# Two feed-forward tiles side by side in the opening wave instead of three, with weights loaded earlier and three pieces of work spread later

## The chip, the cores and the metric

The kernel runs on one NeuronCore of a Trainium2 chip. The metric is the time of one execution in microseconds (us) on the device; the time before is the median of three runs.

Engines are named as the profile names them: PE is TensorE (matmuls), PEld its weight load, DVE is VectorE, ACT is ScalarE, POOL is GpSimd, SP is SyncE, which here only issues DMAs. A name with a q (SPq, ACTq) is the engine's queue of instructions that wait, branch or issue.

## The reference

One layer of a diffusion backbone over 256 latent and 256 context tokens of width 2048, all in float32:

```python
mod = silu(c) @ w_ada + b_ada              # 9 chunks of 2048; the same for the context's condition
x   = x   + 0.5 * gate * swiglu(rms_norm(x)   * (1 + scale) + shift, w_ffn1_up, w_ffn1_down)
ctx = ctx + 0.5 * gate * swiglu(rms_norm(ctx) * (1 + scale) + shift, w_ffn1_up, w_ffn1_down)
h   = modulate(rms_norm(x), ...)           # and the same for ctx
q, k, v, hy = split(h @ w_in);  kc, vc from the context
attn = softmax(rope(q) [kc; k]^T) [vc; v]  # 8 query heads, 2 key heads of 128
hyo  = hyena(hy, filters)                  # short conv, gate, long conv by an implicit filter, gate
x   = x + gate * concat(rms_norm(attn), rms_norm(hyo)) @ w_out
x   = x + 0.5 * gate * swiglu(modulate(rms_norm(x)), w_ffn2_up, w_ffn2_down)
```

The feed-forward width is 5632. The hyena filters come from a small sine network and are used by their spectrum.

## The kernel before

**Arithmetic.** A float32 product is made of three matmuls in a shorter float format: every operand is split into a high and a low part (`hi`, `lo`), and hi x hi, hi x lo and lo x hi are summed in PSUM (`mm3`). `weight` loads a piece of 0.5 MB into `raw` by SP's queue (four buffers), ACT casts it to `whi` (L199) and DVE makes `wlo` = raw - whi (L201); `whi` and `wlo` have three buffers each. One piece of `up` is 24 matmuls of 512 columns (256 latent and 256 context tokens side by side).

**Order.** The framework puts the instructions of each engine in an order by a planner with its own costs, starting from the order in which the program states them; `tc.issue_after(x)` forces an instruction behind another. The engines then run their orders and wait for each other by semaphores. DMAs issued by SP stand in SP's order, so one that waits for a free buffer holds up those behind it.

**The start.** The tokens `xs` (16 loads) are squared on ACT and summed on DVE; PE sums over partitions (L244), DVE and ACT make 1/rms (`rstd_from`, with a Sqrt on ACT, L231, ahead of which ACT loads a function table), and `spread_row` puts it into all partitions (L255 to L257). `keep_awake` runs matmuls without use meanwhile. The shift and scale of the first feed-forward come from PE: `ada_row(d)` loads 2 MB of `w_ada` for d-tile d (128 of the 2048 columns) into `wrow` (four buffers of 1 MB), multiplies (L163), and `ada_col(d)` copies the row (L170), turns it (L173) and writes the two columns of `mod` (L175, L177).

**The wave.** There are 44 ff tiles of 128 columns. The first `WAVE` = 3 run side by side, because their input `h` comes into being d-tile by d-tile: for d = 0 to 15, `ada_row(d + 2)`, `ada_col(d + 1)`, `wave_h(d)` (L523 on DVE, L525 on ACT for hi, L527 on DVE for lo), then six matmuls (L208 to L210) for each of the three tiles. Their pieces of weights are loaded at d = 0, 4, 8 and 12, when they are needed. The third tile's two PSUM banks come from the `pb` pool, in which the banks of `ada_row` and of the filter also lie. Between the tiles `next(steps)` runs pieces of `filter_spectrum`: three layers of the sine network (matmul L379, DVE L381 to L386, Sin on ACT L388), then four blocks of 256 channels (Exp L414, matmul L417, L418 to L431 on DVE with Abs on ACT L425, L434 to L439, spectrum L445 to L450).

**After the wave.** `f1.up(j)` runs the other ff tiles one by one in four pieces, and after each four of them `f1.down` adds their part of the output. Behind each piece `ada_hook` puts products for the other chunks of the modulation on DVE (`ada_dve`, L136), which need the condition rows `crow`; these are loaded by SP and put through Silu right behind the wave.

**Mixing.** The last `down` runs first for the context tokens, then for the latents; `mix_input` makes the inputs of the projections meanwhile, driven by the hook and by `KV_PLAN`: `rstd_steps` squares (L266) and, one step on, makes 1/rms and spreads it together with the first `h`. Later `group_in` splits the outputs of attention and hyena for the output projection and sums their squares; `out_unit(g, b)` multiplies group g by a quarter of the output's columns, and `out_add` multiplies by 1/rms and the gate (L955) and adds to the stream (L956). The hyena group's `group_in` stands as a whole behind the first unit. Behind the last unit, 16 matmuls without use keep PE awake, and the second feed-forward's input is normed and turned (L1005).

Of the kernel before, what the change touches and what calls it, by code (L numbers as in the profile page):

```python
# [18 lines left out]
P = 128  # L19
D = 2048  # L20
# [11 lines left out]
WAVE = 3  # L32
# [21 lines left out]
def hybrid_layer_kernel(ctx: ExitStack, tc: tile.TileContext, a):  # L54
# [137 lines left out]
    def weight(src, shape, eng=None, behind=None):  # L192
        raw = T(wp, shape, "raw", bufs=4)
        load = nc.sync.dma_start(raw, src)
        if done[0]:
            last_load[0] = load
        hi = T(wp, shape, "whi", F32R, 3)
        lo = T(wp, shape, "wlo", F32R, 3)
        S.copy(hi, raw)  # L199
        if behind is None:  # L200
            (eng or V).tensor_sub(lo, raw, hi.bitcast(F32))  # L201
        else:
            with tc.issue_after(behind.ins):
                V.tensor_sub(lo, raw, hi.bitcast(F32))
# [32 lines left out]
    def row_rstd(tiles, n, y, between=None):  # L237


# [7 lines left out]
        with ExitStack() as order:  # L247
            if between:
                with tc.issue_after(last.ins):
                    order.enter_context(tc.issue_after(between().ins))  # L250
            return spread_row(nt, r_, y)

    def spread_row(nt, r_, y):
# [5 lines left out]
    def rstd_steps(pairs, n, y):  # L259

        todo_, acc = [], None
        for q, t in enumerate(pairs):
            last = q == len(pairs) - 1
            sq = (tmp if last or acc is not None else tmp2)((P, 2, L))
            for part in ((0, 1) if last else (slice(0, 2),)):
                S.activation(sq[:, part, :], t[:, part, :], AF.Square)  # L266
            if last:
                todo_.append(sq)
# [6 lines left out]
        row_rstd([[t_[:, j, t * P : (t + 1) * P] for t_ in todo_ for j in range(2)] for t in range(2)], n, y)  # L275
# [22 lines left out]
    class Ffn:  # L298
# [12 lines left out]
        def piece(self, j, kq, ps2, eng=None):  # L311
            whi, wlo = weight(self.wup[j, kq], (P, 4, 2, P), eng)
# [181 lines left out]
    for i in range(2):  # L494
        for q, t in enumerate(xs[i]):
            sq = U((P, 2, L))
            S.activation(sq, t, AF.Square)
            if q:
                last_sq = V.tensor_add(accs[i], accs[i], sq)
            else:  # L500
                accs.append(sq)
    spin = PA()
# [11 lines left out]
    with tc.issue_after(last_sq.ins):  # L514
        with tc.issue_after(awake.ins):
            spread = row_rstd([[accs[i][:, j, t * P : (t + 1) * P] for j in range(2)] for i in range(2) for t in range(2)],
                     D, rs.rearrange("p i l -> p (i l)"), lambda: ada_row(0))
# [26 lines left out]
    for d in range(KT):  # L544
# [6 lines left out]
        for j in range(WAVE):  # L551
            if d and d % 4 == 0:
                w[j] = weight(f1.wup[j, d // 4], (P, 4, 2, P))
            mm = f1.tile(d, d % 4, w[j], wave[j])
            with ExitStack() as first:
# [3 lines left out]
                if j < 2 or d < 3:  # L559
                    next(steps, None)  # L560
    for _ in steps:
        pass
# [5 lines left out]
    crow = [T(adap, (P, D), f"crow{i}", bufs=1) for i in range(2)]  # L568
    for i in range(2):
        nc.sync.dma_start(crow[i], a["crow"][i : i + 1, :].partition_broadcast(P))  # L570
        S.activation(crow[i], crow[i], AF.Silu)
    f1.hook = ada_hook
# [601 lines left out]
```

## Time and profile before

| | |
|---|---|
| median of 3 runs | 2696.45 us (2695.83 to 2697.5) |
| profiled execution | 2693.7 us, span from first to last instruction 2691.9 us |
| mean granted clock of PE | 0.997 of full speed |
| PE busy | 2661.5 us (99%) |
| DVE busy | 1715.6 us (64%) |
| ACT busy | 940.8 us (35%) |
| moved by DMA | 515.43 MB, mean 191 GB/s |

The profile shows one execution. Busy times of PE are modelled and overlap from one matmul to the next, so the distance from start to start says more than the length of one. A wait is the idle time of an engine ahead of an instruction, named by what it waited for last.

### The profile page before, as it was taken

To read this page: it belongs to the slowest core of one execution; us is meant where nothing else is said; L and a number is where in the kernel's file an instruction comes from. 1 tells how busy PE (TensorE), PEld (TensorE's weight loads), DVE (VectorE), ACT (ScalarE), POOL (GpSimd) and SP (SyncE) were. 2 spreads that over 40 slices of the span, in tenths; PEclk is the share of its full clock that TensorE was granted. 3 is DMA by queue.
4 is the path that set the end of the run, shared out by engine and by line. 5 is a ranking of instruction groups with operands and counts; after the bars stand their busy time and mean duration, and the time that the engine had idled before them with its cause. 6 is when DMAs were issued, how large, how long until landed. Compare 5 with 4: busy or idle time off the path is not lost.

```text
span 2691.9 us, 32590 instructions
## 1 busy us (share of the span) xinstructions
PE 2661.5 (99%) x12588; PEld 2187.1 (81%) x12588; DVE 1715.6 (64%) x2687; ACT 940.8 (35%) x1217; POOL 1.0 (0%) x7
## 2 busy tenths in 40 slices
PE   9999999999999999999999999999999999999999
PEld 6678888888888888888888878888888888888887
DVE  5589898976696767443333697788665555554444
ACT  4343222222222222222222455456454444444333
POOL 0000000000000000000000000000000000000000
PEclk9999999999999999999999999999999999999999
DMA  9776666666686665522322455334645555556664
GB/s 368 299 271 216 217 212 229 206 232 212 221 296 235 204 229 208 188 99 94 101 95 95 133 165 188 125 110 157 194 163 190 188 188 189 190 191 203 200 200 157
DMA packets 145395, 515.43 MB, mean 191 GB/s; under 512 B 17303, under 2 KB 21336, under 8 KB 140888
## 3 DMA queue, kind: packets, MB, share of 16 engines
q1 hardware_dynamic: 143464, 510.60, 55.7%
q10 hardware_dynamic: 1776, 2.75, 0.3%
q8 instruction: 99, 1.62, 0.2%
q14 instruction: 56, 0.46, 0.1%
HBM read 509.07 MB, written 4.21 MB: 191 GB/s over the span
## 4 chain that ended last, share of the span: by engine, by line
PE 95%; DVE 3%; DMA 1%; issue 0%; ACT 0%; SPq 0%; ACTq 0%; DVEq 0%
PE pa L210 12%; PE pa L209 12%; PE pa L208 11%; PE pa L940 10%; PE pa L939 10%; PE pa L938 10%; PE pb L208 7%; PE pb L210 7%; PE pb L209 7%; PE pa L216 3%; PE pa L218 2%; PE pb L163 1%; PE pa L652 1%; PE pa L653 1%; PE pa L651 1%; DVE wlo L201 1%
## 5 line engine op out<-in xcount | busy, mean ns | idle before, releaser
L201 DVE TENSOR_TENSOR wlo<-raw,whi 128x1024 fp32r<-128x1024 f32 x645 | 788.1, 1223 | 674.1 <-ACT whi L199 661.6
L199 ACT CAST whi<-raw 128x1024 fp32r<-128x1024 f32 x648 | 681.1, 1052 | 1360.6 <-PE pa L209 495.2
L210 PE MATMUL pa<-u,wlo 128*128 128x512 f32 x1376 | 535.7, 390 | 2.7 <-DVE wlo L201 2.7
L208 PE MATMUL pa<-u,whi 128*128 128x512 f32 x1376 | 536.9, 391 | 1.0 <-ACT u L525 0.9
L209 PE MATMUL pa<-u,whi 128*128 128x512 f32 x1376 | 536.8, 390 | 0.8 <-DVE u L527 0.8
L939 PE MATMUL pa<-wlo,u 128*128 128x512 f32 x1072 | 418.5, 390 | 1.9 <-DVE wlo L201 1.9
L938 PE MATMUL pa<-whi,u 128*128 128x512 f32 x1072 | 419.9, 392 | 0.3 <-ACT u L1010 0.3
L940 PE MATMUL pa<-whi,u 128*128 128x512 f32 x1072 | 418.5, 391 | 0.0
L208 PEld LDWEIGHTS pa<-u,whi 128*128 128x128 f32 x1376 | 258.0, 188 | 58.4 <-issue 3.9
L210 PEld LDWEIGHTS pa<-u,wlo 128*128 128x128 f32 x1376 | 258.1, 188 | 57.3 <-DVE wlo L201 3.8
L209 PEld LDWEIGHTS pa<-u,whi 128*128 128x128 f32 x1376 | 258.4, 188 | 56.7 <-DVE u L527 2.1
L208 PE MATMUL pb<-u,whi 128*128 128x512 f32 (+1 forms) x800 | 299.3, 375 | 0.0
L209 PE MATMUL pb<-u,whi 128*128 128x512 f32 (+1 forms) x800 | 298.1, 373 | 0.0
L210 PE MATMUL pb<-u,wlo 128*128 128x512 f32 (+1 forms) x800 | 298.1, 373 | 0.0
L939 PEld LDWEIGHTS pa<-wlo,u 128*128 128x128 f32 x1072 | 201.8, 188 | 43.1 <-DVE wlo L201 2.0
L940 PEld LDWEIGHTS pa<-whi,u 128*128 128x128 f32 x1072 | 201.5, 188 | 43.0 <-DVE u L1012 1.0
L938 PEld LDWEIGHTS pa<-whi,u 128*128 128x128 f32 x1072 | 201.6, 188 | 41.9 <-ACT u L1010 0.6
L136 DVE CUSTOM_DVE_ANT_0 adas<-adaw,crow,mod 128x1024 bf16<-128x1024 f32 x160 | 205.0, 1281 | 25.4 <-DMA adaw<-in_w_adaT_dram 22.9
L136 DVE CUSTOM_DVE_ANT_0 adas<-adaw,crow,bada 128x1024 bf16<-128x1024 f32 x160 | 204.9, 1280 | 18.0 <-DMA adaw<-in_w_adaT_dram 15.9
L208 PEld LDWEIGHTS pb<-u,whi 128*128 128x128 f32 x800 | 151.2, 189 | 31.0 <-issue 4.8
L210 PEld LDWEIGHTS pb<-u,wlo 128*128 128x128 f32 x800 | 151.2, 189 | 26.9 <-issue 0.8
L209 PEld LDWEIGHTS pb<-u,whi 128*128 128x128 f32 x800 | 151.2, 189 | 26.1
(237 smaller groups left out, 2096.9 us busy)
## 6 DMA issues: line engine op xcount, KB each, us to landing
raw<-in_w_up_dram SPq DMA_DIRECT2D x352, 512.0 KB, 3.3
adaw<-in_w_adaT_dram SPq DMA_DIRECT2D x223, 512.0 KB, 5.1
raw<-in_w_dn_dram SPq DMA_DIRECT2D x184, 512.0 KB, 3.8
wrow<-in_w_ada_dram SPq DMA_DIRECT2D x32, 1024.0 KB, 7.4
raw<-in_w_hy_dram SPq DMA_DIRECT2D x32, 512.0 KB, 3.3
raw<-in_w_o_dram SPq DMA_DIRECT2D x32, 512.0 KB, 4.0
raw<-in_w_kv_dram SPq DMA_DIRECT2D x16, 512.0 KB, 3.7
raw<-in_w_q_dram SPq DMA_DIRECT2D x16, 512.0 KB, 3.3
```

Of the source, the lines that this page charges most:

```text
L136: V.tensor_tensor_reduce(out=sc, in0=t, in1=crow[i][:, b * (D // 2) : (b + 1) * (D // 2)], scale=1.0, scalar=mcol if b else bada[:, n : n ...
L163: last = PE.matmul(bank[g : g + 32, 0 : 2 * P], cs[:, k, :], t[:, k8, :], start=k < 4, stop=k >= KT - 4)
L199: S.copy(hi, raw)
L201: (eng or V).tensor_sub(lo, raw, hi.bitcast(F32))
L208: PE.matmul(ps, w[0], xx[0], start=start, stop=False)
L209: PE.matmul(ps, w[0], xx[1], start=False, stop=False)
L210: return PE.matmul(ps, w[1], xx[0], start=False, stop=stop)
L216: PE.matmul(ps, w[0], x, start=start, stop=stop)
L218: PE.matmul(ps[:, 0, :], w[1], x[:, 0, :], start=False, stop=False)
L938: PE.matmul(ps[t], hi, w[0], start=start, stop=False)
L939: PE.matmul(ps[t], hi, w[1], start=False, stop=False)
L940: last = PE.matmul(ps[t], lo, w[0], start=False, stop=stop)
```

## The change

`WAVE` becomes 2: the third ff tile is made by `f1.up(2)` behind the wave. The weights of the wave's next four d-tiles are loaded into `raw` at the end of d = 1, 5 and 9 (`weight_load`), and `weight` takes them from there at d = 4, 8 and 12. The filter keeps its number of steps: one behind each tile, and one more behind the second tile while d < 3. The condition rows are loaded behind `up(2)`, by ACT's queue, and the hook is set there. `row_rstd` is divided into `token_rstd` (sums and 1/rms) and `spread_row`; in `rstd_steps` a `yield` lies between them, so that the generator has one step more, and one `next(more)` is added before the hook takes over. `root_table` puts a Sqrt of one column behind the last square, so that ACT loads its table there. `group_in` becomes a generator of four steps, and the hyena group's steps stand one behind each of the four units. In `out_unit`, the last of the four pieces finishes token tile 0 before token tile 1, and `out_add` puts token tile 1's product behind token tile 0's sum.

```diff
--- before.py
+++ after.py
@@ -29,7 +29,7 @@
 UPG = FF // 256
 CT = HW // P
 EPS = 1e-6
-WAVE = 3
+WAVE = 2
 ADA_RATE = 1.25
 FILTER_J = 36
 GATE_J = 20
@@ -189,16 +189,21 @@
         V.tensor_sub(lo, src, hi.bitcast(F32))
         return hi, lo
 
-    def weight(src, shape, eng=None, behind=None):
+    def weight_load(src, shape):
         raw = T(wp, shape, "raw", bufs=4)
         load = nc.sync.dma_start(raw, src)
         if done[0]:
             last_load[0] = load
+        return raw
+
+    def weight(src, shape, behind=None, raw=None):
+        if raw is None:
+            raw = weight_load(src, shape)
         hi = T(wp, shape, "whi", F32R, 3)
         lo = T(wp, shape, "wlo", F32R, 3)
         S.copy(hi, raw)
         if behind is None:
-            (eng or V).tensor_sub(lo, raw, hi.bitcast(F32))
+            V.tensor_sub(lo, raw, hi.bitcast(F32))
         else:
             with tc.issue_after(behind.ins):
                 V.tensor_sub(lo, raw, hi.bitcast(F32))
@@ -234,8 +239,12 @@
         V.scalar_tensor_tensor(e, e, -0.5, m, op0=ALU.mult, op1=ALU.mult)
         return V.scalar_tensor_tensor(y, e, 1.5, y, op0=ALU.add, op1=ALU.mult)
 
-    def row_rstd(tiles, n, y, between=None):
-
+    def root_table(behind):
+
+        with tc.issue_after(behind.ins):
+            S.activation(tiny((P, 1)), ones[:, 0:1], AF.Sqrt)
+
+    def token_rstd(tiles, n):
 
         nt = len(tiles)
         ps = PB((P, nt, 2))
@@ -244,13 +253,11 @@
                 last = PE.matmul(ps[:, t, :], blk, ones[:, 0:2], start=q == 0, stop=q == len(blocks) - 1)
         r_ = tiny((P, nt))
         rstd_from(ps[:, :, 0], n, (P, nt), tiny, r_)
-        with ExitStack() as order:
-            if between:
-                with tc.issue_after(last.ins):
-                    order.enter_context(tc.issue_after(between().ins))
-            return spread_row(nt, r_, y)
-
-    def spread_row(nt, r_, y):
+        return r_, last
+
+    def spread_row(r_, y):
+
+        nt = r_.shape[1]
         dg, row = tmp2((P, nt, P)), PB((P, nt * P))
         V.tensor_mul(dg, ident.unsqueeze(1).broadcast_to((P, nt, P)), r_.unsqueeze(2).broadcast_to((P, nt, P)))
         PE.matmul(row, ones, dg.rearrange("p a b -> p (a b)"), start=True, stop=True)
@@ -263,8 +270,9 @@
             last = q == len(pairs) - 1
             sq = (tmp if last or acc is not None else tmp2)((P, 2, L))
             for part in ((0, 1) if last else (slice(0, 2),)):
-                S.activation(sq[:, part, :], t[:, part, :], AF.Square)
+                square = S.activation(sq[:, part, :], t[:, part, :], AF.Square)
             if last:
+                root_table(square)
                 todo_.append(sq)
             elif acc is None:
                 acc = sq
@@ -272,7 +280,9 @@
             else:
                 V.tensor_add(acc, acc, sq)
         yield
-        row_rstd([[t_[:, j, t * P : (t + 1) * P] for t_ in todo_ for j in range(2)] for t in range(2)], n, y)
+        r_, _ = token_rstd([[t_[:, j, t * P : (t + 1) * P] for t_ in todo_ for j in range(2)] for t in range(2)], n)
+        yield
+        spread_row(r_, y)
 
     def modulated(i, d, rs, cm, hi, lo):
 
@@ -308,8 +318,8 @@
             f = PB if alt else PA
             return f((P, 2, L)), f((P, 2, L))
 
-        def piece(self, j, kq, ps2, eng=None):
-            whi, wlo = weight(self.wup[j, kq], (P, 4, 2, P), eng)
+        def piece(self, j, kq, ps2):
+            whi, wlo = weight(self.wup[j, kq], (P, 4, 2, P))
             for k4 in range(4):
                 self.tile(kq * 4 + k4, k4, (whi, wlo), ps2)
             self.hook()
@@ -494,11 +504,12 @@
     for i in range(2):
         for q, t in enumerate(xs[i]):
             sq = U((P, 2, L))
-            S.activation(sq, t, AF.Square)
+            square = S.activation(sq, t, AF.Square)
             if q:
                 last_sq = V.tensor_add(accs[i], accs[i], sq)
             else:
                 accs.append(sq)
+    root_table(square)
     spin = PA()
 
     def keep_awake(n, behind=None):
@@ -511,10 +522,12 @@
         return last
 
     awake = keep_awake(AWAKE[0])
-    with tc.issue_after(last_sq.ins):
-        with tc.issue_after(awake.ins):
-            spread = row_rstd([[accs[i][:, j, t * P : (t + 1) * P] for j in range(2)] for i in range(2) for t in range(2)],
-                     D, rs.rearrange("p i l -> p (i l)"), lambda: ada_row(0))
+    with tc.issue_after(last_sq.ins), tc.issue_after(awake.ins):
+        r_, last = token_rstd([[accs[i][:, j, t * P : (t + 1) * P] for j in range(2)] for i in range(2) for t in range(2)], D)
+    with tc.issue_after(last.ins):
+        last = ada_row(0)
+    with tc.issue_after(last.ins):
+        spread = spread_row(r_, rs.rearrange("p i l -> p (i l)"))
 
     def wave_h(d):
         hi, lo = U((P, 2, L), F32R), U((P, 2, L), F32R)
@@ -550,14 +563,17 @@
             wave_h(d)
         for j in range(WAVE):
             if d and d % 4 == 0:
-                w[j] = weight(f1.wup[j, d // 4], (P, 4, 2, P))
+                w[j] = weight(None, (P, 4, 2, P), raw=raws[j])
             mm = f1.tile(d, d % 4, w[j], wave[j])
             with ExitStack() as first:
                 if d == j == 0:
                     first.enter_context(tc.issue_after(mm.ins))
                     ada_row(ahead)
-                if j < 2 or d < 3:
+                next(steps, None)
+                if d < 3 and j:
                     next(steps, None)
+        if d % 4 == 1 and d // 4 < 3:
+            raws = [weight_load(f1.wup[j, d // 4 + 1], (P, 4, 2, P)) for j in range(WAVE)]
     for _ in steps:
         pass
     for j in range(WAVE):
@@ -565,14 +581,16 @@
     rowp_cm.__exit__(None, None, None)
     adap_cm = tc.tile_pool(name="adap", bufs=2)
     adap = adap_cm.__enter__()
-    crow = [T(adap, (P, D), f"crow{i}", bufs=1) for i in range(2)]
-    for i in range(2):
-        nc.sync.dma_start(crow[i], a["crow"][i : i + 1, :].partition_broadcast(P))
-        S.activation(crow[i], crow[i], AF.Silu)
-    f1.hook = ada_hook
+    crow = []
 
     for j in range(WAVE, FILTER_J):
         f1.up(j)
+        if j == WAVE:
+            for i in range(2):
+                crow.append(T(adap, (P, D), f"crow{i}", bufs=1))
+                nc.scalar.dma_start(crow[i], a["crow"][i : i + 1, :].partition_broadcast(P))
+                S.activation(crow[i], crow[i], AF.Silu)
+            f1.hook = ada_hook
         if j % GRP == 0:
             f1.down(j // GRP - 1)
             if j == GATE_J:
@@ -628,6 +646,7 @@
         yield from normed_from(i, rs1[:, i, :], 3, out)
 
     more = mix_input(1, cont)
+    next(more)
     f1.hook = lambda: next(more)
     f1.down(JT // GRP - 1, 0, residual)
 
@@ -914,13 +933,13 @@
                 S.activation(hl[:, 0, :], src[i][:, j, :], AF.Copy, scale=gout[:, k : k + 1])
                 V.scalar_tensor_tensor(hl[:, 1, :], src[i][:, j, :], gout[:, k : k + 1], hl[:, 0, :].bitcast(F32),
                                        op0=ALU.mult, op1=ALU.subtract)
-            sq = (tmp2 if i == 0 else tmp)((P, 2, L))
+            sq = U((P, 2, L)) if i == 0 else tmp((P, 2, L))
             S.activation(sq, src[i], AF.Square)
             if acc is None:
                 acc = sq
             else:
                 V.tensor_add(acc, acc, sq)
-        return acc
+            yield acc
 
     def group_rstd(acc):
         ps = PB((P, 2, 2))
@@ -944,27 +963,31 @@
         ps = [PA(), PA()]
         for kp in range(4):
             whi, wlo = weight(a["w_o"][b, 4 * g + kp], (P, 2, 512))
-            for k2 in range(2):
+            for t, k2 in ((0, 0), (1, 0), (0, 1), (1, 1)) if kp < 3 else ((0, 0), (0, 1), (1, 0), (1, 1)):
                 k = 2 * kp + k2
-                last = tok_mm(ps, [y[8 * g + k][:, s, :] for s in range(2)], (whi[:, k2, :], wlo[:, k2, :]), k == 0, k == 7)
+                last = tok_mm(ps, [y[8 * g + k][:, s, :] for s in range(2)], (whi[:, k2, :], wlo[:, k2, :]), k == 0, k == 7, (t,))
         return ps, last
 
     def out_add(ps, r_, b):
         for t in range(2):
             o = tmp2((P, 512))
-            V.scalar_tensor_tensor(o, ps[t], r_[:, t : t + 1], grow[b], op0=ALU.mult, op1=ALU.mult)
-            V.tensor_add(xt[t][b], xt[t][b], o)
-
-    acc = group_in(attnT, 0)
+            with ExitStack() as order:
+                if t:
+                    order.enter_context(tc.issue_after(last.ins))
+                V.scalar_tensor_tensor(o, ps[t], r_[:, t : t + 1], grow[b], op0=ALU.mult, op1=ALU.mult)
+            last = V.tensor_add(xt[t][b], xt[t][b], o)
+        return last
+
+    for acc in group_in(attnT, 0):
+        pass
     for _ in gate:
         pass
     grow = gate_row(0)
     ra = group_rstd(acc)
-    acch = None
+    hy_in = group_in(hyT, CT)
     for b in range(NB):
         ps, _ = out_unit(0, b)
-        if b == 0:
-            acch = group_in(hyT, CT)
+        acch = next(hy_in)
         out_add(ps, ra, b)
     rh = group_rstd(acch)
     sumsq = bada1[:, 0 : 2 * NB].rearrange("p (t b) -> p t b", b=NB)
```

## Rows read from the trace of the kernel before

**Rows 1.** Page, the chain that ended last: shares of the span

```profile
PE 95%; DVE 3%; DMA 1%; issue 0%; ACT 0%; SPq 0%; ACTq 0%; DVEq 0%
```

**Rows 2.** Windows: stretch, engines' busy us (x instructions), PE's clock, DMA share, GB/s

```profile
0.00:30.00 30.00, 26.45 (x153) 20.38 (x154) 14.86 (x35) 16.39 (x27) 0.95 (x7) 0.89 0.97 371
30.00:180.00 150.00, 142.27 (x924) 91.80 (x924) 95.80 (x237) 59.53 (x100) 0.00 (x0) 1.00 0.82 301
180.00:1500.00 1320.00, 1320.00 (x5826) 1093.45 (x5825) 868.50 (x1369) 308.27 (x355) 0.00 (x0) 1.00 0.55 190
```

**Rows 3.** Waits of PE: waiting line, releaser: total us, times, longest

```profile
PE pa L210 <- DVE wlo L201: 2.7, 2, 1.5
PE pb L173 <- ACT sg L170: 2.5, 2, 2.0
PE pb L256 <- DVE sg L255: 2.5, 1, 2.5
...
PE pa L939 <- DVE wlo L201: 1.9, 1, 1.9
...
PE pb L1005 <- DVE u L999: 1.6, 1, 1.6
...
PE pa L208 <- ACT u L525: 0.9, 2, 0.7
```

**Rows 4.** Windows, the two stretches of half clock in mixing

```profile
1868.75:1872.16 3.41, 3.41 (x10) 2.64 (x9) 1.94 (x3) 0.00 (x0) 0.00 (x0) 0.50 0.65 198
1534.24:1537.66 3.42, 2.87 (x11) 2.70 (x12) 1.66 (x6) 1.06 (x3) 0.00 (x0) 0.50 0.45 153
```

**Rows 5.** Around d = 4: DVE's timeline (start, us, line), and a window

```profile
73.87 2.29 DVE L201 TENSOR_TENSOR wlo<-raw,whi 128x1024 fp32r<-128x1024 f32 x2
...
63.00:80.00 17.00, 13.18 (x90) 8.12 (x89) 14.48 (x34) 7.96 (x14) 0.00 (x0) 1.00 0.71 287
```

**Rows 6.** Timelines of DVE, ACT and PE, d = 0 to 3

```profile
29.44 3.49 DVE L204 TENSOR_TENSOR wlo<-raw,whi 128x1024 fp32r<-128x1024 f32 x3
...
37.84 0.42 ACT L388 ACTIVATE u<-mt 64x256 f32<-64x256 f32 x1 [5.36 <-DVE mt L386]
...
39.02 0.91 ACT L525 ACTIVATE u<-sq,mod 128x256 fp32r<-128x256 f32 x2
...
47.67 0.91 ACT L525 ACTIVATE u<-sq,mod 128x256 fp32r<-128x256 f32 x2
...
48.63 1.21 PE L208 MATMUL pa<-u,whi 128*128 128x512 f32 x4
...
55.79 0.89 ACT L525 ACTIVATE u<-sq,mod 128x256 fp32r<-128x256 f32 x2
...
57.52 0.50 PE L208 MATMUL pa<-u,whi 128*128 128x512 f32 x1
```

**Rows 7.** Timelines of ACT and PE behind a filter block's first L417

```profile
97.68 0.49 ACT L525 ACTIVATE u<-sq,mod 128x256 fp32r<-128x256 f32 x1
...
98.98 0.71 PE L208 MATMUL pa<-u,whi 128*128 128x512 f32 x2
```

**Rows 8.** Mixing input: ACT's timeline, and a window

```profile
1531.57 1.28 ACT L231 ACT_TABLE_LOAD   x1
...
1544.00:1592.00 48.00, 43.73 (x247) 37.28 (x247) 47.03 (x92) 30.56 (x53) 0.00 (x0) 1.00 0.47 149
```

**Rows 9.** Output projection's beginning: DVE's timeline, and a window

```profile
1863.04 0.88 DVE L915 SCALAR_TENSOR_TENSOR u<-u,gout,u 128x256 fp32r<-128x256 f32 x2
1863.83 0.69 DVE L922 TENSOR_TENSOR sg<-sg,sq 128x512 f32<-128x512 f32 x1
...
1844.00:1870.00 26.00, 24.06 (x125) 20.49 (x124) 25.35 (x49) 19.92 (x33) 0.00 (x0) 0.98 0.41 132
```

**Rows 10.** The last unit's product and sum: DVE's timeline

```profile
1945.56 1.40 DVE L955 SCALAR_TENSOR_TENSOR sg<-pa,small,u 128x512 f32<-128x512 f32 x2
1946.88 1.28 DVE L956 TENSOR_TENSOR u<-u,sg 128x512 f32<-128x512 f32 x2
```

## The prediction

> **What bounds the kernel now.** I read the chain that ended last, then the busy times by stage, the waits of PE, and the timelines around each long wait. The chain is PE for 95% of the span [rows 1]. From 180 to 1500 us PE is busy without a gap, and nearly all of it is matmuls of 512 columns: 1320 us / 5826 = 0.227 us each [rows 2]. So a matmul that is only moved costs the same at its new place; the time can change only where PE waits or runs at half clock. The reader is to see that these places are few [rows 3]: 2.7 + 2.5 us on `wlo` and `sg` and 0.9 us on `u`, nearly all before 180 us; 2.5 us before L256 of the mixing input; 1.9 us in the output projection; 1.6 us ahead of L1005. [...] DMA is busy 82% of 30 to 180 us at 301 GB/s, against 371 GB/s in the first 30 us [rows 2].
>
> **The third tile leaves the wave.** Its 16 x 6 = 96 matmuls, 96 x 0.227 = 21.8 us, go from the wave into `up(2)` behind it. There they run at full rate: DVE has one `wlo` of 1.15 us [rows 5] for 24 matmuls (5.4 us), and no hook yet. So the wave must get shorter by 21.8 us for no change, 6 x 0.227 = 1.36 us in each d-tile. Where a d-tile is held by its own chain on DVE and ACT, those 1.36 us turn into waiting.
>
> d = 1 to 3: `h` of the next d-tile goes through ACT's L525, and that stands behind the filter's Sin, L388: Sin starts at 37.84, L525 at 39.02 [rows 6]. For d = 2, L525 ends at 48.58 and PE starts the tile at 48.63 [rows 6]: no slack. For d = 1 the second wait of L208 on L525 (0.9 in all less 0.7) says the same [rows 3]. For d = 3, L525 ends at 56.68 and PE comes at 57.52 [rows 6], slack 0.84. So 1.36 + 1.36 + 0.52 = 3.2 us come back as waits. Ahead of this chain DVE makes two `wlo` instead of three, 3.49 / 3 = 1.16 us less [rows 6]. Sum +2.1; bounds 0 (the planner fills it) and 3 x 1.36 = 4.1.
>
> d = 4: PE waits 2.0 us on `sg` and 1.2 us on `wlo` [rows 3] while DVE is busy 14.5 of 17 us [rows 5]. DVE sets the pace, and PE's 2 x 1.36 = 2.7 us (tiles of d = 3 and d = 4) are not won by themselves. DVE loses one `wlo` (1.15), and another can be made before, since two tiles leave the third `whi` and `wlo` buffer free and the raw weight is there three d-tiles earlier: 2.7 - 2.3 = +0.4. Bounds: -3.2 (both waits go) and +2.7. I take +0.5. The early raw loads pass two row transfers on SP's queue; I cost that at nothing, since the wave then moves some 2 MB less out of 301 x 150 = 45 MB. If the wave lasts 130 us that is 43 / 130 = 331 GB/s, below the 371 seen.
>
> d = 5 to 14: no wait of PE is listed there. The tightest place that I found returns once in each of the last three filter blocks: L525 is ready at 98.17 and PE comes at 98.98 [rows 7], slack 0.81, so 1.36 - 0.81 = 0.55, three times: +1.7. Bounds 0 and 11 x 1.36 = 15; I take the small one, since no PE wait stands there.
>
> The end of the wave: PE waits 0.7 us for L525 and 1.5 us for `wlo` (the longest of their rows [rows 3]), with DVE on the first ada products. Now the condition rows and the hook come one ff tile later, so `wlo` is no longer behind them; L525 is still behind the filter's last copy, with three matmuls (0.7) less before it. 2.2 before, 1.4 after: -0.8; bounds -2.2 and +1. The row loads now stand in ACT's queue, their two Silu before the following casts. ACT is busy 308 of 1320 us there [rows 2] and the weights are two pieces (10.9 us) ahead, so I cost them at nothing; without that cover one transfer, some 5 us, would show once. The hooks per piece and the ada work stay the same. The third tile's two banks of the `pb` pool also come free; I count nothing for that.
>
> Front: 2.1 + 0.5 + 1.7 - 0.8 = +3.5.
>
> **1/rms and the Sqrt table.** In the start, `spread_row` still stands behind `ada_row(0)` on PE, so the table's earlier load gains nothing there; a bound is its 1.28 us [rows 8]. In the mixing input, sums and spread now have one piece of `down` between them, and the table load leaves the chain. At stake: the 2.5 us wait [rows 3] and 1.7 us of half clock [rows 4], 4.2 together. But the sums now come one piece earlier, right behind the last residual, and from 1544 on DVE is busy 47.0 of 48 us [rows 8], so that only what DVE wins stays won. I take a little over half, -2.3; bounds 0 and -4.2. The load starts at 1531.57 and takes 1.28 us; the wait cannot lose more than that by the hoist alone. [...]
>
> **Hyena inputs.** DVE is busy 25.4 of 26 us to 1870 [rows 9]; PE then waits 1.9 us for `wlo` [rows 3] and runs 3.4 us at half clock [rows 4]. Three of four input steps move to later units: 3 x (0.88 + 0.69) = 4.7 us of DVE [rows 9], more than the wait. Later units are 48 matmuls, 10.9 us, against 4 x 1.15 + 2.68 = 7.3 us of DVE work, so 1.6 more fits. -3.6; bounds 0 and -3.6. If the squares were late, the next in line would be `group_rstd`'s matmuls, L929.
>
> **Token order in the last piece.** Token tile 0 is finished six matmuls (1.36 us) earlier, and its product and sum, 0.70 + 0.64 us [rows 10], run under tile 1's matmuls. The wait before L1005 is 1.6 [rows 3]: -1.3; bounds 0 and -1.6.
>
> Sum: +3.5 - 2.3 - 3.6 - 1.3 = -3.7 us. The profiled execution took 2693.7 us (span 2691.9), which becomes 2690.0. The median of the runs is 2696.45, 2.75 above it, so I predict 2696.45 - 3.7 = **2692.7**. A measurement of this kernel tells about 0.2%, 5.4 us, from no change.
>
> **Rivals.**
> *The cover is not missed.* The planner reorders matmuls, and with free buffers and banks the waits of d = 4 and of the wave's end go: front -(2.0 + 1.2 + 2.2) + 2.1 = -3.3, in all -10.5: 2686.0. For it: no wait from d = 5 to 14. Against it: DVE stays full around d = 4.
> *The wave is held by its chains (slower).* Every d-tile, not three, hangs on the filter's work in ACT's and DVE's order, so that the 1.36 us come back 16 times: 21.8 less the wave end's 2.2, and -7.2 from the middle: +12.4, 2708.9. It decides for slower from (7.2 + 5.4) / 1.36 = 9 to 10 d-tiles on. For it: `h` of d = 1, whose L525 waits behind Sin. Against it: the slack of 0.8 and the empty wait list. [...]
> *The middle does not come.* The sums wait for the squares and the clock still falls; hyena steps are only pushed: +3.5 - 1.3 = +2.2, 2698.7.
>
> **How the numbers follow.** Forecast 0.50 (its own range 2688 to 2697; 0.20 of it under -5.4, 0.30 within), cover not missed 0.22 (faster), chains 0.13 (0.12 slower, 0.01 within), middle fails 0.15 (within). Faster 0.42, same 0.46, slower 0.12. The range takes the forecast's, the first rival's middle and the third rival's with a little beyond: 2686 to 2700; the chains' rival is left out, and the lower part of the first.
>
> **What would show it.** `up(2)` with matmuls every 0.227 us and no wait; about 18 us less until the wave's last tile; new short waits on L525 at d = 1 to 3 and after L417; a granted clock of 1.0 around 1534 and 1869 (moved by the shift) and no wait on `wlo` there; a wait of about 0.3 us before L1005. The prediction is wrong if waits of a microsecond appear in most d-tiles, if `up(2)` waits on `whi`, or if PE waits for the mixing sums.

## The result and the profile after

The changed kernel takes **2705.35 us** (median of 6 runs, 2704.95 to 2709.13) against 2696.3 for the kernel before beside it (6 runs, 2695.81 to 2697.5): ratio 1.0036, 95% interval 1.0023 to 1.0049. It is slower by 9 us. I had forecast 2692.7 and a range of 2686 to 2700: outside, and of the other sign. The rival whose time came nearest is "the wave is held by its chains", 2708.9. The profiled execution took 2709.13 (span 2707.3), 3.8 above its median, that of before 2.75 below its own, so the two traces differ by 15.4 where the medians differ by 9. The surplus is at least in part half clock: the mean granted clock of this execution is 0.992, that of four of the six runs 0.994.

Windows of the changed kernel, columns as in [rows 2]; the first two answer to [rows 2], the others cut the wave into four:

```profile
30.00:180.00 150.00, 136.13 (x852) 84.03 (x851) 86.02 (x222) 55.35 (x95) 0.00 (x0) 0.91 0.79 289
180.00:1500.00 1320.00, 1320.00 (x5825) 1093.38 (x5824) 873.69 (x1379) 308.53 (x356) 0.00 (x0) 1.00 0.55 190
30.00:60.00 30.00, 24.88 (x178) 14.21 (x176) 17.69 (x54) 7.03 (x15) 0.00 (x0) 0.87 1.03 380
60.00:100.00 40.00, 35.83 (x227) 20.59 (x223) 20.20 (x55) 16.19 (x29) 0.00 (x0) 0.88 0.73 257
100.00:140.00 40.00, 37.96 (x253) 23.01 (x254) 23.76 (x60) 12.13 (x22) 0.00 (x0) 0.91 0.80 292
140.00:180.00 40.00, 37.46 (x201) 26.22 (x200) 24.36 (x54) 20.00 (x29) 0.00 (x0) 0.96 0.67 250
```

From 180 to 1500 nothing differs: the third tile's matmuls run there at 0.227 us. But for 2.4 us at the very end, this trace's loss lies in 30 to 180: 852 matmul instructions where before had 924, PE busy 6 us less, and a granted clock of 0.91 where [rows 2] had 1.00. Before had no half clock in the wave at all.

The waits of PE, as in [rows 3]:

```profile
PE pa L213 <- ACT u L538: 9.5, 5, 3.3
...
PE pb L1028 <- DVE u L1022: 2.7, 1, 2.7
PE pa L671 <- DVE wlo L206: 2.6, 3, 1.9
PE pb L389 <- ACT u L398: 2.4, 1, 2.4
...
PE pb L948 <- DVE u L941: 1.3, 1, 1.3
...
PE pb L263 <- DVE sg L262: 1.1, 1, 1.1
```

L213 on L538 is what L208 on L525 was in [rows 3]: 0.9 us in two waits became 9.5 in five. The waits on `sg` and `wlo` of d = 4 are gone or small. PE's timeline, the waiting rows of the wave:

```profile
41.16 0.64 PE L389 MATMUL pb<-u,u 64*64 64x256 f32 x2 [2.39 <-ACT u L398]
...
56.71 1.65 PE L213 MATMUL pa<-u,whi 128*128 128x512 f32 x3 [2.03 <-ACT u L538]
70.49 0.79 PE L213 MATMUL pa<-u,whi 128*128 128x512 f32 x1 [3.26 <-ACT u L538]
...
124.14 2.08 PE L213 MATMUL pa<-u,whi 128*128 128x512 f32 x4 [2.04 <-ACT u L538]
...
166.98 0.50 PE L213 MATMUL pa<-u,whi 128*128 128x512 f32 x1 [2.05 <-ACT u L538]
```

ACT's timeline ahead of the longest one:

```profile
65.15 1.28 ACT L424 ACT_TABLE_LOAD   x1
...
68.21 0.49 ACT L538 ACTIVATE u<-sq,mod 128x256 fp32r<-128x256 f32 x1
69.41 0.63 ACT L435 ACTIVATE u<-u 128x512 f32<-128x512 f32 x1 [0.71 <-DVE u L433]
69.94 0.49 ACT L538 ACTIVATE u<-sq,mod 128x256 fp32r<-128x256 f32 x1
```

The second half of `h` stands in ACT's order behind the filter's L435, which itself waits for DVE: the chain that I had seen for d = 1, now at d = 4. (Counted by L213's matmuls, the waits at 56.71, 70.49 and 124.14 are those of d = 3, 4 and 10, and 166.98 is d = 15, the end of the wave; the expectation of e5 calls the first two d = 2 and 3.) And with these waits the clock falls. Windows (the same columns) of three of these stretches, of one with only 0.54 us of wait ahead of it, and of the place where [rows 4] had its first, moved by the shift:

```profile
42.20:45.60 3.40, 3.40 (x20) 1.61 (x20) 2.98 (x9) 0.58 (x2) 0.00 (x0) 0.50 1.01 414
55.80:62.60 6.80, 5.89 (x25) 3.40 (x26) 1.67 (x4) 1.62 (x4) 0.00 (x0) 0.50 0.82 297
69.50:76.30 6.80, 5.81 (x23) 2.72 (x24) 1.15 (x3) 2.11 (x5) 0.00 (x0) 0.50 0.81 304
100.20:103.60 3.40, 3.40 (x20) 1.28 (x19) 3.29 (x8) 1.57 (x2) 0.00 (x0) 0.50 0.84 352
...
1882.00:1889.00 7.00, 7.00 (x32) 5.81 (x31) 5.99 (x9) 3.13 (x3) 0.00 (x0) 1.00 0.59 181
```

In the stretch at 55.80 matmuls of 512 columns start 0.43 us apart (61.60, 62.03, 62.46), right behind it 0.23 (62.78, 63.01, 63.24), so nearly half of such a stretch is lost. With the stretches at 124.1 and 168.4 the wave has 27.2 us of half clock, a loss of at most 13.6 (PE is busy for 25.3 of them); its PE waits are 13.8 us where before had 7.4. Together that is at most 20 us. By the places of the matmuls, 16.6 of the 21.8 us that left the wave came back in it.

### The profile page after: what moved, and what is told of

Same layout as the page of the kernel before. It is cut to its first block, busy times and chain, and to the rows that moved or that the text cites. A ratio compares the mean times of both kernels' runs of the same rounds, so it can differ in the third digit from the quotient of the medians.

```text
span 2707.3 us, 32573 instructions
## 1 busy us (share of the span) xinstructions
PE 2673.1 (99%) x12588; PEld 2193.5 (81%) x12588; DVE 1716.0 (63%) x2687; ACT 941.5 (35%) x1220; POOL 1.0 (0%) x7
## 4 chain that ended last, share of the span: by engine, by line
PE 96%; DVE 3%; ACT 1%; DMA 0%; issue 0%; SPq 0%; ACTq 0%; DVEq 0%
PE pa L213 12%; PE pa L214 12%; PE pa L215 12%; PE pa L957 10%; PE pa L959 10%; PE pa L958 10%; PE pb L213 6%; PE pb L215 6%; PE pb L214 6%; PE pa L221 3%; PE pa L223 1%; PE pb L163 1%; PE pa L671 1%; PE pa L672 1%; PE pa L670 1%; PE pb L455 1%
## 5 line engine op out<-in xcount | busy, mean ns | idle before, releaser
L213 PE MATMUL pa<-u,whi 128*128 128x512 f32 x1408 | 550.4, 393 | 9.5 <-ACT u L538 9.5
L214 PE MATMUL pa<-u,whi 128*128 128x512 f32 x1408 | 552.0, 392 | 1.1 <-DVE u L540 1.1
L215 PE MATMUL pa<-u,wlo 128*128 128x512 f32 x1408 | 551.0, 391 | 0.0
L213 PEld LDWEIGHTS pa<-u,whi 128*128 128x128 f32 x1408 | 265.6, 189 | 71.1 <-ACT u L538 11.1
L214 PEld LDWEIGHTS pa<-u,whi 128*128 128x128 f32 x1408 | 265.8, 189 | 62.0 <-issue 3.8
L215 PEld LDWEIGHTS pa<-u,wlo 128*128 128x128 f32 x1408 | 265.7, 189 | 56.0 <-issue 1.2
L213 PE MATMUL pb<-u,whi 128*128 128x512 f32 (+1 forms) x768 | 286.1, 373 | 0.0
L214 PE MATMUL pb<-u,whi 128*128 128x512 f32 (+1 forms) x768 | 285.7, 372 | 0.0
L215 PE MATMUL pb<-u,wlo 128*128 128x512 f32 (+1 forms) x768 | 285.6, 372 | 0.0
L213 PEld LDWEIGHTS pb<-u,whi 128*128 128x128 f32 x768 | 145.3, 189 | 25.1 <-ACT u L183 0.2
L214 PEld LDWEIGHTS pb<-u,whi 128*128 128x128 f32 x768 | 145.4, 189 | 25.0
L215 PEld LDWEIGHTS pb<-u,wlo 128*128 128x128 f32 x768 | 145.4, 189 | 24.9
```

The source lines that it names most:

```text
L213: PE.matmul(ps, w[0], xx[0], start=start, stop=False)
L214: PE.matmul(ps, w[0], xx[1], start=False, stop=False)
L215: return PE.matmul(ps, w[1], xx[0], start=False, stop=stop)
```

## Experiments

Theory A: two tiles are too little work of PE to cover the making of the next d-tile's `h` and the filter's steps. Rival B: the early raw loads cost, by pushing the row loads back. Rival C: the loss lies behind the wave. Each group of runs shares its runs of the kernel before, whose medians were 2696.5, 2697.6, 2696.4, 2697.7 and 2698.1; so a difference of 1 to 2 us between runs of two groups tells little.

**e1: two tiles alone,** on the kernel before.

```diff
-WAVE = 3
+WAVE = 2
...
-                if j < 2 or d < 3:
-                    next(steps, None)
+                next(steps, None)
+                if d < 3 and j:
+                    next(steps, None)
...
         f1.up(j)
+        if j == WAVE:
+            f1.hook = ada_hook
```

> The kernel before with two tiles side by side in the wave (its weights loaded when needed, as before; the hook starts behind the third tile) and nothing else of the change. Theory A, lost cover: with two tiles PE reaches each d-tile before its input h, waits, and its clock falls; the wave loses 14 to 17 of the 21.8 us that the third tile costs behind it, and the kernel takes 2703 to 2712 us. Rival B, the early raw loads push the row loads back: without them the wave loses 3 us or less, 2697 to 2700 us. Rival C, it lies behind the wave (condition rows, sums, hyena inputs): 2696 to 2699 us.

2705.41 us, ratio 1.0034 (1.0022 to 1.0047).

**e2: the rest with three tiles,** on the changed kernel: `WAVE = 3`, the old rule for steps, condition rows right behind the wave.

> The changed kernel with three tiles side by side again, all else of the change kept (weights three d-tiles ahead; condition rows by ACT's queue, but right behind the wave; sums, hyena inputs and token order as changed). Theory A, lost cover: the wave's loss goes, 2692 to 2697 us, that is the time before and what the later edits give. Rival B, early loads: still 2702 us or more, since three pieces are now loaded early. Rival C: 2703 to 2706 us.

2701.81, ratio 1.0019 (1.0010 to 1.0028). So each part loses by itself: A and B both live, though B had asked for 2702 or more.

**e3: the changed kernel with useless matmuls** in a spare bank.

```diff
+    fill_bank = PB()
...
+        for _ in range(6):
+            PE.matmul(fill_bank[:, 0:P], ones, ones, start=True, stop=True)
```

> The changed kernel with six matmuls of 128 columns without use (12 passes of 0.11 us, 1.3 us) behind the second tile of every d-tile, in the place of the third tile. [...] Theory A in the form that the waits alone count: no change, 2704 to 2707 us. Rival B, early loads hold the rows back: 2705 us or more, the waits as they are.

2706.77, ratio 1.0039 (1.0026 to 1.0052); for a fallen clock as the larger part I had written 2695 to 2701. The waits of the wave fall from 13.8 to 2.0 us and its half clock from 27.2 to 0, 25.4 us together at most; the filler's 192 records take about 22.7, an estimate (36 of them took 4.26). The idle time was filled and the clock held, but the useless work cost about what it saved.

**e4: `h` one d-tile ahead,** on the changed kernel: its instructions for d + 1 are issued before the filter's steps of d.

```diff
     ada_col(1)
+    wave_h(1)
     for d in range(KT):
...
                 ada_col(d + ahead - 1)
-            wave_h(d)
+                wave_h(d + 1)
```

> The changed kernel with the input h of the wave made one d-tile earlier, so that it stands ahead of that d-tile's filter steps on ACT and DVE. [...] Rival B, the rows come late: h waits for the same rows, 2703 to 2707 us. Rival C: 2704 to 2706 us.

2693.43, ratio 0.9986 (0.9978 to 0.9995): 12 us below the changed kernel, and below the kernel before. By theory A, with PE's waits on `h` gone and the granted clock kept, I had written 2689 to 2697. Its window of the wave, and then the row of PE's waits that is on `h`:

```profile
30.00:180.00 150.00, 142.26 (x922) 90.28 (x920) 95.75 (x237) 59.89 (x101) 0.00 (x0) 1.00 0.86 311
```

```profile
PE pa L213 <- ACT u L538: 5.1, 5, 1.5
```

Five waits remain, but the longest is 1.5 us, and the clock stays at 1.00. Theory A is shown for this part.

**e5 and e6: late loads.** The weights of d = 4, 8, 12 are loaded when needed again, in the changed kernel (e5) and in e2 (e6).

```diff
-                w[j] = weight(None, (P, 4, 2, P), raw=raws[j])
+                w[j] = weight(f1.wup[j, d // 4], (P, 4, 2, P))
...
-        if d % 4 == 1 and d // 4 < 3:
-            raws = [weight_load(f1.wup[j, d // 4 + 1], (P, 4, 2, P)) for j in range(WAVE)]
```

> The changed kernel with the wave's next weights loaded when they are needed again (d = 4, 8, 12), all else as changed. Theory A (two tiles are too little cover for the next d-tile's h): the waits on u L536-L538 and the half clock in the wave stay; what two tiles alone cost was 9 us (2705.4), and the middle's edits give back about 3, so 2700 to 2704. Theory B (the early loads push the row loads back or turn PE's planned order): with three tiles the rest cost 5 us; those go here too, so at most 2700, and the first waits on u of d = 2 and 3 (2.0 and 3.3 us) are gone or under 1 us.

> Three tiles in the wave as before, and of the change only what is left without the early loads: the condition rows by ACT's queue, 1/rms in two halves, the hyena steps, the token order. Theory B (the early loads made the 5 us that the rest cost with three tiles): 2693 to 2696, the wave within 2 us of before's, no wait of 3.3 us on u. Rival C (something else of the rest did it, the earlier Sqrt table or the condition rows): 2700 to 2702, as with the early loads.

e5 2698.5, ratio 1.0009 (1.0001 to 1.0018); e6 2694.08, 0.9994 (0.9984 to 1.0004). So the early loads cost 2705.35 - 2698.5 = 6.9 us with two tiles and 2701.81 - 2694.08 = 7.7 with three; the third tile's leaving costs 2698.5 - 2694.08 = 4.4. The time of e5 is in theory B's range, below theory A's: the early loads were the larger part. B's other sign did not come: in e5's profiled execution, 6.0 us above its median, L213 still waits 3.0 us on L538.

**e7: e6 with `h` ahead** (the edit of e4). **e8: e4 with the output projection's old token order.**

```diff
-            for t, k2 in ((0, 0), (1, 0), (0, 1), (1, 1)) if kp < 3 else ((0, 0), (0, 1), (1, 0), (1, 1)):
+            for k2 in range(2):
...
-            with ExitStack() as order:
-                if t:
-                    order.enter_context(tc.issue_after(last.ins))
```

> The same with h of d+1 made one d-tile earlier, as in the run with two tiles that reached 2693.4. Theory A (h's chain is what PE waits for, and three tiles cover it but for 0.9 us of waits and their clock): 1 to 3 us below the same without it, 2690 to 2694. Rival: three tiles hide h wholly, and the earlier h only fills DVE's and ACT's queues ahead of the filter: no gain or up to 3 us slower.

> Two tiles with h one d-tile ahead (2693.4), and the output projection's token order as before. Theory (the new order let a weight's remainder of 1.2 us on DVE slip between the last product and the last sum, so that the wait ahead of the transposes is 2.7 instead of 1.6 us): the wait is 1.6 us again and 1 to 2 us are won, 2691 to 2692.5. Rival (the wait comes from elsewhere and the token order is worth its 1.3 us): the wait is 2.7 or more, 2693.5 to 2695.

e7 2685.19, 0.9959 (0.9945 to 0.9972), 8.9 below e6, far more than expected: the wave's waits fall from 8.3 to 3.8 us and its half clock from 13.8 us to none. (e6's profiled execution is 5.6 above its median, so part of that is the execution's own.) e8 2690.43, 3.0 below e4. What changed, DVE's timeline at the last unit shows, first of the changed kernel, then of e8, and under it e8's wait of PE ahead of the transposes:

```profile
1960.02 0.74 DVE L977 SCALAR_TENSOR_TENSOR sg<-pa,small,u 128x512 f32<-128x512 f32 x1
1960.68 1.22 DVE L206 TENSOR_TENSOR wlo<-raw,whi 128x1024 fp32r<-128x1024 f32 x1
1961.81 0.68 DVE L978 TENSOR_TENSOR u<-u,sg 128x512 f32<-128x512 f32 x1
```

```profile
1942.24 1.40 DVE L975 SCALAR_TENSOR_TENSOR sg<-pa,small,u 128x512 f32<-128x512 f32 x2
1943.56 1.28 DVE L976 TENSOR_TENSOR u<-u,sg 128x512 f32<-128x512 f32 x2
1944.76 1.22 DVE L206 TENSOR_TENSOR wlo<-raw,whi 128x1024 fp32r<-128x1024 f32 x1
```

```profile
PE pb L1026 <- DVE u L1020: 1.6, 1, 1.6
```

With the new order a weight's remainder, 1.2 us, which nothing needs yet, slips between tile 1's product and its sum; the wait ahead of the transposes is 2.7 with it and 1.6 without, as in [rows 3, 10]. That is 1.1 of the 3.0 us. Behind the wait e4 then runs 3.4 us at half clock, a loss of 1.7 at most, and e8 doesn't; the windows, first of e4, then of e8:

```profile
1951.70:1955.10 3.40, 3.38 (x8) 2.70 (x9) 3.19 (x8) 1.58 (x3) 0.00 (x0) 0.50 0.00 0
```

```profile
1949.30:1952.70 3.40, 3.40 (x14) 2.43 (x15) 3.19 (x8) 1.62 (x4) 0.00 (x0) 1.00 0.00 0
```

Of the profiled executions with the new order all but e10's have this stretch, of those with the old order none.

**e9 and e10: a part of the early loads.** e9 loads only d = 4 late, e10 only d = 8 and 12.

> The changed kernel with only the first of the three early loads (the weights of d = 4, two tiles) issued when needed; those of d = 8 and 12 stay three d-tiles early. Theory B1 (from 30 to 60 us the 16 DMA engines are full, 1.02 to 1.04 of the stretch in the changed kernel, so a megabyte ahead of the row loads makes the rows late, and later there is room): all of the 7 us come back, 2697 to 2700. Rival B2 (it is the planned order of PE, DVE and ACT that the early loads turn, at every one of the three places): a third comes back, 2702 to 2704.

> The other half: only the first load early (d = 4), those of d = 8 and 12 when needed. Theory B1: the loss stays, 2703 to 2706. Rival B2: a third of it stays, 2699.5 to 2702.

e9 2702.8, ratio 1.0022; e10 2701.05, 1.0018. The first load costs 2.5 us by e10 (2701.05 - 2698.5), the two later ones 4.3 by e9: the first place and the two later ones each have a share, not only the stretch where the DMA engines are full. B1, by which the first alone would bring all back, falls.

**e11: e7 with the old token order. e12: that with the mixing input's 1/rms as before.**

```diff
     more = mix_input(1, cont)
-    next(more)
...
-                root_table(square)
...
-        yield
         spread_row(r_, y)
```

> Three tiles in the wave, weights loaded when needed, h one d-tile ahead (2685.2), and the output projection's old token order. If the order's 3.0 us add to it: 2681.5 to 2683. Rival (the clock falls elsewhere in exchange): 2684 to 2686.

> The same with the mixing input's 1/rms undone: no earlier Sqrt table there, sums and spread in one piece of work, the first squares not ahead of the last down. My prediction put this edit at 2.3 us: 2684 to 2685 then. By the places of the matmuls with three tiles it won 0.8 us: 2682.5 to 2683.5. If the clock falls once more or once less there: 1.7 us to either side.

e11 2681.3 (0.9946, 0.9933 to 0.9958), the fastest of all, 3.9 below e7. e12 2685.86: the mixing edit wins 4.6, where I had written 2.3 and 0.8, and 1.7 to either side for the clock; 10.2 us of half clock behind 1500 in e12's profile are none in e11's. The three longest waits of the wave in e11, and two windows of it:

```profile
PE pa L213 <- ACT whi L204: 1.0, 1, 1.0
PE pb L173 <- ACT sg L170: 0.7, 1, 0.7
PE pb L163 <- PE pb L173: 0.7, 1, 0.7
```

```profile
30.00:180.00 150.00, 147.23 (x951) 98.16 (x950) 89.87 (x224) 61.30 (x101) 0.00 (x0) 0.99 0.80 301
...
1500.00:1960.00 460.00, 448.31 (x2467) 382.55 (x2467) 374.61 (x701) 257.09 (x409) 0.00 (x0) 1.00 0.45 155
```

**e13: the early loads by POOL's queue** instead of SP's. **e14: e11 with early loads. e15: e11 with two tiles. e16: the kernel before with `h` ahead.**

> The changed kernel with its early loads issued by POOL's queue instead of SP's; the order of PE stays nearly that of the changed kernel. If the loss comes from the row loads behind them on SP's queue: most of the 6.9 us comes back, 2698 to 2701. If it comes from the order of PE, DVE and ACT, or from the shared DMA engines: 2703.5 to 2707.

> The best kernel so far (2681.3: three tiles, late loads, h one d-tile ahead, old token order) with the early loads put in. If they cost by making h late (its chain has no slack), h ahead takes the cost away: 2680 to 2683. If they cost by the row loads or by what follows them on PE itself: 2685 to 2689.

> The best kernel so far with two tiles in the wave instead of three, loads late. Theory A (the third tile was the cover for h alone): with h ahead it is hardly missed, 2681 to 2684. Rival (the cover is needed for the row loads and the filter's chains too): the 4.4 us that the third tile was worth without h ahead stay, 2685 to 2687.

> The kernel before with h made one d-tile ahead, and nothing of the change. If the gain of 8.9 us (2694.1 to 2685.2 with the rest of the change, loads late) is its own: 2686 to 2689. If it came only together with the earlier Sqrt table or the condition rows on ACT's queue: 2692 to 2697.

e13 2702.12, ratio 1.0018: half of the loss back, between the two expectations. I had expected its order of PE to stay nearly that of the changed kernel; it differs from 49.18 us on, so e13 moves the queue and the order together. e14 2689.83, 8.5 above e11; e15 2690.79, 9.5 above. Both are above all that I had written for them: with `h` ahead either change still costs, and both together (e8) no more, 9.1. So `h` was not all that the cover was for. In e14 PE again waits 1.96 us on L538 at 62.97, with the row products late in PE's order (none of them waits for a row there); the longest wave wait in e15 is 2.6 on the filter's L441. e16 2691.33, 0.9978 (0.9969 to 0.9988): between its two expectations; 6.4 us are the edit's own.

**e18 and e17: the late-loading e5 with the six early transfers put in as useless ones,** on POOL's queue (e18) and on SP's (e17).

```diff
+        if d % 4 == 1 and d // 4 < 3:
+            for j in range(WAVE):
+                nc.gpsimd.dma_start(T(wp, (P, 4, 2, P), "raw", bufs=4), f1.wup[j, d // 4 + 1])
```

> The changed kernel with late loads (2698.5), and the six early transfers of 512 KB put in once more as useless ones, on POOL's queue; the order of PE, DVE and ACT is the same as without them. If the early loads cost by taking the DMA engines from the row loads: 2703 to 2706. If they cost by the order that is planned around them: 2697.5 to 2699.5.

> The same with the useless transfers on SP's queue, ahead of the row loads as in the change. If the DMA engines' load is the cause: as on POOL's queue. If only SP's queue matters (the rows stand behind them): 2703 to 2706 here and 2697.5 to 2699.5 on POOL's. If the order that is planned for the weights' consumers is the cause: 2697.5 to 2700 on both.

e18 2702.49, ratio 1.0014, between what I had written for it; e17 2712.18, 1.0052 (1.0038 to 1.0065), far above the 2706 that I had allowed it. Nearly all of e18's 4 us lies ahead of the wave. Its timelines of POOL's queue, SP's queue and PE, and under them the same two of e5:

```profile
1.47 1.20 POOL L577 DMA_DIRECT2D raw<-in_w_up_dram  x2
14.81 1.01 SPq L159 DMA_DIRECT2D wrow<-in_w_ada_dram  x2
34.52 0.48 PE L213 MATMUL pa<-u,whi 128*128 128x512 f32 x1
```

```profile
12.26 1.69 SPq L159 DMA_DIRECT2D wrow<-in_w_ada_dram  x3
30.90 0.48 PE L213 MATMUL pa<-u,whi 128*128 128x512 f32 x1
```

POOL has nothing else to do, so its first two transfers start at 1.47 us, beside the inputs that the start waits for, and the first tile comes 3.6 us late. If that passes through in full, it leaves 0.4 of the 4 us for the wave, less than the medians tell apart, although four of the six transfers fall in it (34.2, 35.1, 44.9 and 75.1) and its DMA share rose from 0.82 to 0.87. The same bytes on SP's queue cost 13.7. SP's queue in e17:

```profile
102.41 0.33 SPq L159 DMA_DIRECT2D wrow<-in_w_ada_dram  x1
102.79 0.42 SPq L577 DMA_DIRECT2D raw<-in_w_up_dram  x1
...
105.12 0.59 SPq L577 DMA_DIRECT2D raw<-in_w_up_dram  x1
115.00 2.55 SPq L159 DMA_DIRECT2D wrow<-in_w_ada_dram  x3
```

The row load at 115.00 is the 25th; in e18, with nothing useless on this queue, the 25th is issued at 102.23. By the profile it isn't a useless transfer that ends SP's 9.2 us of waiting ahead of it, but the landing of the filter's `spec`. e13's first tile came at 33.51, 2.3 later than the changed kernel's 31.23; without that it would be near 2699.8 by estimate, 1.3 from e5. So the load of the DMA engines is not what costs, and the loss comes with the transfers' places on SP's queue. How it comes about is not shown, since the order planned for PE changes with them: e18's matmuls stand in e5's order, one for one, while e17's leave it at 50.37 us. The weight loads of L163, which take the rows, hardly wait for one, first in the changed kernel, then in e17:

```profile
PEld pb L163 <- DMA wrow<-in_w_ada_dram: 0.7, 1, 0.7
```

```profile
PEld pb L163 <- DMA wrow<-in_w_ada_dram: 0.9, 2, 0.7
```

In e5 it is 0.7 too. That speaks for the planned order and against rows that reach PE late, but no run separates the two.

The runs side by side: us of PE waits from 30 to 180, of half clock from 30 to 190 and from 190 on (both of the profiled execution; half clock is 2 x (1 - mean clock) x length, summed over windows of 10 us), and the median. A row's first three columns are of one execution, so they are to be read along the row rather than subtracted between rows.

```
                                waits  half   half   median
                                30-180 wave   later
before                           7.4    0.0    6.8   2696.3
changed                         13.8   27.2   10.2   2705.4
e1  two tiles alone              9.3   13.6   20.6   2705.4
e2  three tiles, the rest        9.9   13.6    6.8   2701.8
e5  changed, late loads         11.2   23.8   10.2   2698.5
e6  three tiles, late loads      8.3   13.8   10.2   2694.1
e4  changed, h ahead             7.5    0.0   10.2   2693.4
e8  e4, old token order          7.6    3.4    3.4   2690.4
e7  e6, h ahead                  3.8    0.0   10.2   2685.2
e11 e7, old token order          2.7    3.4    0.0   2681.3
e17 e5, useless loads on SP     19.1   20.4   10.2   2712.2
```

## Why the prediction was wrong

*The step that failed first: "The early raw loads pass two row transfers on SP's queue; I cost that at nothing".* They cost 6.9 us (e5), 7.7 with three tiles (e6). My reason was bandwidth, 331 GB/s below 371, over a mean of 150 us. That bandwidth isn't it was right (e18). What I didn't work out is what the transfers are put ahead of on SP's queue, and the order that is planned with them. What is not settled: whether it is the place in the queue itself or the order of PE that is planned with it, since e17 differs from e18 in both; the weight loads, which wait at most 0.9 us for rows in all, speak for the order.

*"The third tile leaves the wave", front +3.5.* Measured +4.4 between e6 and e5, near it; but +8.9 in e1, on the kernel before. The size depends on what stands beside it, and e15's 9.5 says the same. The mechanism was right, `h` behind the filter in ACT's order, but its places were not: of the 1.36, 1.36 and 0.52 forecast for d = 1 to 3 came 0.15, nothing and 2.03, and it held at more places than I had allowed: at d = 4 too, where I had +0.5 from DVE's pace, and at d = 10, where I took "the small one" of 0 to 15. The rows at 69.41 and 69.94 show that order for d = 4: L435 starts after 0.71 us of waiting for DVE, and L538 0.53 us behind it. The two waits of d = 4 did go, as the bound -3.2 said, but 3.26 us on `h` of the same d came in their place; and the wave's end kept a wait of 2.05 where I had 1.4 left. A transfer of condition rows, which I had put at some 5 us, lands 5.7 us after its issue in the kernel before and 7.7 in the changed one, where the Silu waits 1.7 for it.

*What no step had: the half clock in the wave.* I priced dips in the middle from [rows 4], and put new waits into the wave without pricing any there. It costs up to 13.6 us in the profiled execution, about twice what the waits grew by (6.4).

*The middle, -7.2 in all.* 1/rms: -2.3 forecast, -4.6 by e12; but in the changed kernel itself a wait of 1.1 us and a dip at 1547 stayed, and by the places of the matmuls its trace gains only 0.6 there. What a table load costs, the row at 65.15 shows: it takes 1.28 us, and the next activation starts at 66.44, right behind it. Hyena inputs: -3.6 forecast; between the first hyena matmul and the projection's 64th the changed kernel gains 4.0 (3.0 by the projection's end), and the wait on `wlo` and its dip are gone: right, though never run by itself. L948 waits 1.3, but at 1864.61 on the attention's sums, not on the hyena group's, which I had named as next in line. Token order: -1.3 forecast, +3.0 by e8 (+3.9 by e11): wrong sign. I counted DVE's 0.70 + 0.64 as if nothing could stand between, and no half clock behind a longer wait. The 1.7 us for a stretch of half clock, a term of the forecasts for 1/rms and hyena inputs, is half its length, and that no run shows in full: in the first stretch of [rows 4] matmuls start 0.43 us apart (1870.42, 1870.85), right behind it 0.23 (1872.61, 1872.84), by which its 3.41 us lose about 1.6, an estimate.

*`up(2)` with no wait:* right. *About 18 us less until the wave's last tile:* the first matmuls of the last `down` come 16.6 us later in the trace, so of 21.8 about 5 were gained. From there to the end of the output projection the shift falls from 16.6 to 13.0, and then rises to 15.4 with the token order's wait and its half clock. Those 2.4 us apart, the loss doesn't lie behind the wave, and rival C falls. In medians, e6 is 3.5 below its own kernel before, the third tile adds 4.4 and the early loads 6.9: +7.8, beside the 9.0 measured. The forecast missed by 12.7: 6.9 of it are the early loads, 0.9 the third tile (4.4 for 3.5), 3.7 the middle (-3.5 for -7.2), mostly by the token order. That the rival "the wave is held by its chains" came within 3.6 us is partly luck: it had nothing for the early loads and took the whole -7.2.

## What to carry to other kernels

Work that hides a chain can be taken away only where the chain has slack at every turn: look for the producer's place in its engine's order, and issue it one turn earlier first; here that alone was worth 6 to 12 us, more than any gain in the change. It is no full remedy: with `h` ahead the third tile's leaving still cost 9.5. Price a new wait on TensorE with the half clock behind it (in the changed kernel's wave 3.4 or 6.8 us behind waits of 2.0 to 3.3), and a load that is moved forward by what it is put ahead of in its queue and by the order that is then planned, not by bandwidth alone. An edit of order that frees a consumer early also lets other work in: look at what the planner will put into the gap.

## What the hardware showed that I had not expected

In the changed kernel each wait of 2.0 to 3.3 us in the wave went with 3.4 or 6.8 us at a granted clock of 0.50, while with waits of at most 1.5 us (e4) the clock stayed at 1.00 through it. But the wait's length doesn't settle it. The kernel before has one of 2.0 us on `sg` [rows 3], at 70.7, and no half clock in the wave; the changed kernel's stretch at 100.2 has only 0.54 us ahead of it; and e4 and e8, with the same order of PE in the wave, both wait 1.2 us on `h`, at 68.63 and 68.03, and only e8's clock fell. The windows behind that wait, of e4 and then of e8:

```profile
70.70:74.00 3.30, 3.19 (x26) 1.78 (x24) 3.24 (x9) 1.48 (x3) 0.00 (x0) 1.00 1.02 429
```

```profile
70.10:73.40 3.30, 3.30 (x9) 2.57 (x8) 2.44 (x8) 1.48 (x3) 0.00 (x0) 0.50 0.99 420
```

What does settle it is not shown. On POOL's queue, where nothing else stood, e18's first two transfers started at 1.47 us, and SP's next row load came at 14.81 instead of 12.26. With the late start of 3.6 us taken off, the same 3 MB cost 0.4 us on POOL's queue, by estimate, and 13.7 on SP's, where the two starts at 102.79 and 105.12 themselves took 0.42 and 0.59 us. How much of that is the queue and how much the planned order is not shown.
